# Stage one of a hybrid attention layer: later spreading of the norm factors, earlier requests for the weights of the second products, squares in groups, a longer lead for the splits

## The chip, the cores and the metric

The kernel runs on one core of a Trainium2 chip. The metric is the device time of one execution in microseconds (us). Before the change it is 1033.59 us, the median of 3 runs (1033.48 to 1034.7).

## The reference, cut to what matters

One layer is computed (DEPTH is 1): RMS norm, one input projection for query, key, value and gate, two-dimensional neighbourhood attention with a bias, a SiLU gate, an output projection with the residual, and a final RMS norm, for 2048 tokens of width 1024 and 16 heads of 64.

```python
for i in range(DEPTH):
    g, w_in, rpb, w_out = layers[i]
    h = rmsnorm(x, g)
    if i % N_MIXERS == 0:
        o, gate = neighbourhood_mixer(h, w_in, rpb)
    ...
    x = x + (o * jax.nn.silu(gate)) @ w_out
return rmsnorm(x, norm_f)
```

The change lies in the input projection `h @ w_in` for the first 1024 tokens. There `rmsnorm` is not applied to the rows first: the kernel multiplies the raw rows (times the gain `g`), and scales each finished result by its row's norm factor.

## The kernel before

**Three-part products.** Every float32 operand is split into a high part (a rounded copy, made by ScalarE, ACT in the profile) and a low part (the rest, made by VectorE, DVE). A product is then high by high, high by low and low by high on TensorE (PE). The line pairs L422/L423 (`form`, weights), L529/L530 and L526/L527 (`split_to`, the other operand) and L548/L551 (`split_v`) are such splits.

**Seven products for eight.** A product of two 2x2 block matrices is made from seven block products instead of eight (Strassen's scheme in Winograd's form). `us` in `stage_one` lists twelve weight units: four key units (n = 0 to 3), then query and gate in turn (n = 4 to 11). A unit's weights have quarters A11, A12, A21, A22 and sums S1 to S4 of them (`sum_`, L429). The rows' transposed tokens have quarters x11, x12, x21, x22 and the sums T1 to T4. `uses` says which pair each of the products P = 1 to 7 takes: 1 is A11 by x11, 2 is A12 by x21 (called here a second product; it adds to the PSUM bank of P = 1), 6 is S2 by T2, 7 is S3 by T3, 5 is S1 by T1, 4 is A22 by T4, 3 is S4 by x22. A product is 12 matmuls of 128x512 (L440), four blocks by three parts. P = 6, 7 and 4 of a unit add up in one PSUM bank; between them DVE reads the sum so far out of it (`add`, tile `u`, L453), so (n,7) has to wait until that read of (n,6) is done.

**The order in stage one** is written out by hand. `seq` lists the products of units 0 to 5: steps 0 to 3 are P = 1 of units 0 to 3, steps 4 to 7 are P = 2 of units 0 to 3, steps 8 and 9 are P = 1 and steps 10 and 11 are P = 2 of units 4 and 5. From step 12 on, ten steps make one pair of units: (0,6), (1,6), (0,7), (0,5), (1,7), (0,4), (1,5), (0,3), (1,4), (1,3) for the first pair, steps 22 to 31 for the pair (2,3), steps 32 to 41 for (4,5). From step 42 on the units go one by one. `step(i)` writes a product; what a step leaves for the other engines (copies, sums, outputs) stands behind it. `todo`, filled by `on(i, f, ...)`, hangs further work behind step i, and `forms(i + 4)` splits the weights of the coming steps, four steps ahead up to step 33, five and six after that.

**Between the first products** stand the products of the values (`first_values`, L709), the loads and splits of x12, x21, x22, the sums for T1 to T4 (`sums`, L716 to L719, and `sums4`, L724), and the norm factors. Each engine executes its instructions in the order in which they are written, and the DMA queue of SyncE (SP) too: a load that has to wait for a buffer holds up every later load and store on that queue. The SP queue also lets only a limited number of its transfers be under way, since each waits for the transfer eight places ahead of it to have landed.

**The norm factors** come in five pieces for each half c of the 1024 tokens:

- `load_rows` brings the rows in, `square_rows` squares and sums them on ACT (L209, eight instructions for each half).
- `stats` makes the reciprocal roots on DVE, fourteen small instructions (L214 to L218), into `rt` and, halved, `rth`.
- `diagonal` puts them on four diagonals on DVE (`dg`, L225) and splits these (`dgh` on ACT, L228; `dgl` on DVE, L229).
- `spread_rstd` multiplies `dgh` and `dgl` by ones on PE (L234, L235), so that every partition holds all factors, and copies the result to `rb[c]` on ACT (L238).
- `first_out` scales the sum of P = 1 and P = 2 by `rb[0]` on DVE (L353), which also frees that PSUM bank. `out_` adds up the other outputs on DVE (L458) and scales them by `rb[c]` on GpSimd (POOL, L460).

Before the change `spread_rstd(0)` stands behind step 5 and `spread_rstd(1)` behind step 8, so both come ahead of step 12. `evac_v` (L396) takes the value products out of PSUM on ACT, scaled by `rth`, and stores them (L399).

**Buffers.** `ev` is a pool of eight 128x512 tiles that many helpers share: the copies `u1v` of the first value products (L778), four of the rows of c = 1, the four `v` of `evac_v`, and `dg`, `dgh` and `dgl`. A tile can be taken again when its last user is done, which for a stored tile is the landing of the store.

Of the kernel before, what the change touches and what calls it, by code (L numbers as in the profile page):

```python
# [77 lines left out]
def build(ctx, tc, x, xr, xt, wg, bias, w_out, n0, nf, out):  # L78
    nc = tc.nc
# [327 lines left out]
    def seven_products(us, c0, X1, also):  # L407
# [3 lines left out]
        made = [0]  # L411
# [43 lines left out]
        def out_(n, a, c, P, u, then):  # L455
            kind, j = us[n]
            tmp = ev([128, 512], F32, "tmp")
            nc.vector.tensor_tensor(lay(kind, tmp), of(kind, B[n, P]), lay(kind, u), OP.add)  # L458
            if c0 == 0:
                nc.gpsimd.tensor_tensor(tmp, tmp, rb[c], OP.mult)  # L460
            then.append(lambda: give(kind, 2 * j + a, c, tmp))

# [47 lines left out]
        parts = SimpleNamespace(load=load_w, form=form, sum=sum_, product=product, keep=keep, after=after, B=B)  # L510
# [88 lines left out]
    def stage_one():  # L599
# [175 lines left out]
        split("B21", "x21", (0, 1), "x21")  # L775
        for t in range(4):
            u = ev([128, 512], F32, "u1v")
            nc.scalar.activation(u, ps[t], AF.Copy)  # L778
            nc.sync.dma_start(vu1[t], u)
# [4 lines left out]
        for n in range(2):  # L784
            seven.load(n, "A12")
        load_rows(1, range(4), ev)
# [5 lines left out]
        for n in (4, 5):  # L792
            seven.load(n, "A11")
        for k in range(4, 8):
            first_values(k)
            split("B22", "x22", (k - 4,), "x22")
            sums(k - 4)
            if k > 4:
                forms((4, 5, 7)[k - 5])
        square_rows(0, range(8))  # L800
# [4 lines left out]
        square_rows(1, range(4))  # L805
        load_rows(1, range(4, 8), mp)
        step(3)
        for t in range(4):
            evac_v(0, t, ps[t])
        forms(9)  # L810
        diagonal(0)
        split("T1", "x12", (0, 1), -1.0)
        step(4)
        for n in range(2):
            for f in ("A21", "A22"):
                seven.load(n, f)
        split("T1", "x12", (2, 3), -1.0)
        square_rows(1, range(4, 8))
        stats(1)
        step(5)  # L820
        spread_rstd(0)
        forms(11)
        split("T2", "x11", (0, 1))
        step(6)
        split("T2", "x11", (2, 3))
        diagonal(1)
        first_out(0)
        first_out(1)
        step(7)
        seven.sum(0, "S1")  # L830
        seven.sum(0, "S2")
        first_out(2)
        step(8)
        spread_rstd(1)
        forms(12)
        seven.sum(1, "S1")
        seven.sum(1, "S2")
        split("T3", "x22", (0, 1))
        step(9)
        forms(13)  # L840
        split("T3", "x22", (2, 3))
        first_out(3)
        step(10)
        seven.sum(0, "S3")
        seven.sum(1, "S3")
        forms(14)
# [5 lines left out]
        t4(0)  # L852
        step(11)
        t4(1)
        forms(15)
        on(12, t4, 2)
        on(13, t4, 3)
# [3 lines left out]
        def ask_pair(a):  # L861
            spot = mkp([128, 3, 512], F32, "raw")
            for n, f, home in ((a, "A21", spot[:, 0]), (a, "A22", spot[:, 1]), (a, "A11", spot[:, 2]), (a + 1, "A11", None)):
                seven.load(n, f, lp if home is None else lambda *_, home=home: home)

        for a in (2, 4):
            p, b = 5 * a + 2, a + 1
            on(p + 3, ask_pair, a)
            for i, n, f in ((4, b, "A21"), (4, b, "A22"), (5, a, "A12"), (6, b, "A12")):
                on(p + i, seven.load, n, f)  # L870
            for i, n, f in ((6, a, "S1"), (6, a, "S2"), (7, b, "S1"), (7, b, "S2"), (8, a, "S3"), (9, b, "S3"), (12, a, "S4"), (14, b, "S4")):
                on(p + i, seven.sum, n, f)
# [60 lines left out]
        for i in range(2 * E, N):  # L933
            step(i)
            forms(i + (4 if i < C - 8 else 5 if i < C - 5 else 6))
# [922 lines left out]
```

## Time and profile before

The profiled execution took 1033.15 us by its own time; its span on the core is 1031.4 us.

| What | Value |
|---|---|
| median of 3 runs | 1033.59 us |
| profiled execution, its own time | 1033.15 us |
| its span, mean granted TensorE clock | 1031.4 us, 0.990 |
| PE busy | 1003.2 us (97% of the span), 6904 matmuls |
| DVE busy | 781.7 us (76%) |
| ACT busy | 508.1 us (49%) |
| POOL busy | 174.2 us (17%) |

The slices of the page show where PE is not full. Each digit is a tenth of a slice's time, and a slice is 25.8 us; DVE and PEclk, the granted clock, are beside it:

```profile
PE   9779999999999999999999999999999999999997
DVE  5687788998766686667676576678888888777876
PEclk9989999999999999999999999999999999999999
```

Ahead of the last slice only the second and the third have a PE digit below 9, from 26 to 77 us, in stage one. The third also has a granted clock digit below 9.

### The profile page before, as it was taken

To read this page: it belongs to the slowest core of one execution; us is meant where nothing else is said; L and a number is where in the kernel's file an instruction comes from. 1 tells how busy PE (TensorE), PEld (TensorE's weight loads), DVE (VectorE), ACT (ScalarE), POOL (GpSimd) and SP (SyncE) were. 2 spreads that over 40 slices of the span, in tenths; PEclk is the share of its full clock that TensorE was granted. 3 is DMA by queue.
4 is the path that set the end of the run, shared out by engine and by line. 5 is a ranking of instruction groups with operands and counts; after the bars stand their busy time and mean duration, and the time that the engine had idled before them with its cause. 6 is when DMAs were issued, how large, how long until landed. Compare 5 with 4: busy or idle time off the path is not lost. (4 is left out here: it accounts for less than half of the span.)

```text
span 1031.4 us, 19603 instructions
## 1 busy us (share of the span) xinstructions
PE 1003.2 (97%) x6904; PEld 799.9 (78%) x6904; DVE 781.7 (76%) x1732; ACT 508.1 (49%) x1245; POOL 174.2 (17%) x244
## 2 busy tenths in 40 slices
PE   9779999999999999999999999999999999999997
PEld 7558778888888888888888777777777777778875
DVE  5687788998766686667676576678888888777876
ACT  7662234444335442333343466667676757563343
POOL 0001332322200000000000032323333332320100
PEclk9989999999999999999999999999999999999999
DMA  9733325787875946756555788788988679799553
GB/s 297 266 121 123 131 101 175 257 269 240 279 253 164 278 160 179 219 174 220 181 177 192 233 257 259 235 248 274 275 271 262 206 226 288 233 332 379 136 159 102
DMA packets 149834, 227.66 MB, mean 221 GB/s; under 512 B 13608, under 2 KB 65064, under 8 KB 149736
## 3 DMA queue, kind: packets, MB, share of 16 engines
q1 hardware_dynamic: 147864, 223.40, 67.4%
q0 software_dynamic: 1440, 2.62, 1.7%
q8 instruction: 54, 0.88, 0.3%
q14 instruction: 44, 0.36, 0.1%
q10 hardware_dynamic: 432, 0.40, 0.1%
HBM read 160.31 MB, written 66.06 MB: 219 GB/s over the span
## 5 line engine op out<-in xcount | busy, mean ns | idle before, releaser
L1293 POOL TENSOR_SCALAR x<-x,st 128x360 f32<-128x360 f32 (+5 forms) x192 | 106.4, 572 | 527.4 <-DVE st L1286 527.1
L440 PE MATMUL pp<-h,f 128*128 128x512 f32 x576 | 187.3, 392 | 0.0
L440 PE MATMUL pp<-t,f 128*128 128x512 f32 x702 | 172.3, 390 | 4.2 <-DVE u L453 4.2
L440 PEld LDWEIGHTS pp<-t,f 128*128 128x128 f32 x702 | 131.5, 188 | 32.6 <-issue 3.1
L1281 ACT ACTIVATE x<-x,st 128x360 f32<-128x360 f32 (+5 forms) x256 | 134.2, 526 | 26.4 <-DVE st L1275 26.4
L440 PEld LDWEIGHTS pp<-h,f 128*128 128x128 f32 x576 | 109.3, 190 | 22.9
L440 PE MATMUL pp<-l,f 128*128 128x512 f32 x288 | 113.0, 392 | 0.0
L1275 DVE CUSTOM_DVE_ANT_0 x<-s,em 128x360 f32<-128x360 f32 (+5 forms) x256 | 102.5, 454 | 1.8 <-PE s L1266 1.4
L423 DVE TENSOR_TENSOR f<-raw,f 128x512 fp32r<-128x512 f32 x105 | 77.4, 740 | 29.2 <-ACT f L422 25.3
L460 POOL TENSOR_TENSOR tmp<-tmp,rb 128x512 f32<-128x512 f32 x36 | 58.2, 1620 | 227.6 <-DVE tmp L458 103.7
L422 ACT ACTIVATE f<-raw 128x512 fp32r<-128x512 f32 x105 | 63.2, 622 | 53.1 <-DVE raw L429 29.7
L1340 PEld LDWEIGHTS o<-pta,vt 120*64 120x64 f32 (+2 forms) x1024 | 68.7, 137 | 22.7 <-DVE st L1275 15.2
L1340 PE MATMUL o<-pta,vt 120*64 120x192 f32 (+5 forms) x1024 | 83.4, 316 | 0.3 <-issue 0.3
L1310 DVE COPY pta<-ph 120x512 f32<-120x512 f32 (+5 forms) x96 | 56.0, 638 | 32.8 <-PE ph L1321 32.6
L1266 PE MATMUL s<-kt,q 64*64 64x360 f32 (+5 forms) x1024 | 78.7, 420 | 1.2 <-DVE y L1416 1.0
L1312 ACT ACTIVATE pta<-ph 120x512 f32<-120x512 f32 (+5 forms) x96 | 46.8, 558 | 62.5 <-PE ph L1321 62.3
L440 PEld LDWEIGHTS pp<-l,f 128*128 128x128 f32 x288 | 54.8, 190 | 11.6
L1266 PEld LDWEIGHTS s<-kt,q 64*64 64x64 f32 x1024 | 41.5, 131 | 23.1 <-ACT pta L1312 6.1
L594 PE MATMUL pv<-wh,t 128*128 128x512 f32 x176 | 56.2, 389 | 0.0
L440 PE MATMUL pp<-sixths,f 128*128 128x512 f32 x198 | 54.1, 397 | 0.0
L422 ACT ACTIVATE f<-s 128x512 fp32r<-128x512 f32 x42 | 26.2, 624 | 53.8 <-DVE s L429 50.5
L1626 PE MATMUL py<-woh,f 128*128 128x512 f32 x160 | 51.0, 391 | 0.9 <-DVE y L1416 0.9
(218 smaller groups left out, 1876.1 us busy)
## 6 DMA issues: line engine op xcount, KB each, us to landing
raw<-in_wg_dram SPq DMA_DIRECT2D x124, 256.0 KB, 4.9
row<-in_xr_dram SPq DMA_DIRECT2D x32, 256.0 KB, 5.1
vd<-v SPq DMA_DIRECT2D x32, 256.0 KB, 3.4
sgd<-sg SPq DMA_DIRECT2D x32, 256.0 KB, 4.4
q<-qd SPq DMA_DIRECT2D x32, 256.0 KB, 5.4
sgt<-sgd SPq DMA_DIRECT2D x32, 256.0 KB, 6.6
ogd<-og SPq DMA_DIRECT2D x32, 256.0 KB, 3.3
kt<-kd SPq DMA_DIRECT2D x16, 480.0 KB, 6.7
```

The source lines that it names most:

```text
L422: nc.scalar.activation(t[:, 0], src, AF.Copy)
L423: nc.vector.tensor_tensor(t[:, 1], src, t[:, 0].bitcast(F32), OP.subtract)
L440: nc.tensor.matmul(B[n, P], t[:, int(m == 2), c], x[k][int(m == 1)], start=P in (1, 6, 5) and k == 0 and m == 0, stop=k == 3 and m == 2, s ...
L460: nc.gpsimd.tensor_tensor(tmp, tmp, rb[c], OP.mult)
L594: nc.tensor.matmul(p, a[:, o], b, start=P in (1, 6, 5) and k == 0 and m == 0, stop=k == 3 and m == 2, skip_group_check=True)
L1266: nc.tensor.matmul(pst[s][h * 64:h * 64 + 64], qt[a, g * 64:g * 64 + 64], kt[a, :r1 - r0, c0:c0 + 8 * WIDE[C]].rearrange("p r (s c) -> p s ...
L1275: nc.vector.tensor_tensor_reduce(X[i, C][s], pst[s], EM[p, ROW_TYPE[T]][C > 0][s], -1.0, 1e38, OP.add, OP.min, st[:, o:o + 1])
L1281: nc.scalar.activation(X[i, C][s], X[i, C][s], AF.Exp, bias=st[:, o:o + 1], scale=-1.0, accum_out=st[:, 4 + o:5 + o])
L1293: nc.gpsimd.tensor_scalar(X[i, C][s], X[i, C][s], st[:, o:o + 1], 1.0, op0=OP.mult, op1=OP.mult)
L1310: nc.vector.tensor_copy(o, i_)
L1340: nc.tensor.matmul(o[s * 64:s * 64 + 64, g0 * 64:g1 * 64], vt[:k, strip, s * 64:s * 64 + 64], t[:k, n * 64:(n + g1 - g0) * 64], start=stri ...
L1626: nc.tensor.matmul(B[m, P], t[:, a, c], b, start=P in (1, 6, 5) and k == 0 and i == 0, stop=k == 3 and i == 2, skip_group_check=True)
```

## The change

The diff moves calls in the hand-written order; no arithmetic is added or left out.

- `load` of A12 of units 0 and 1 goes ahead of the stores of `u1v` and of the rows' loads; the rows of c = 1 are asked for behind the A12 and A11 of units 2 to 5, the first six instead of the first four.
- The squares of c = 0 are written in two groups of four among the sums of x12 and x22. The squares of c = 1 go behind `diagonal(0)`, behind steps 4 and 5.
- `spread_rstd(0)` goes from behind step 5 to behind step 8, three products later. `spread_rstd(1)` goes from behind step 8 to behind step 15. One output of step 15 that needs `rb[1]` is held until step 16 (`held`, `scale_held`).
- `stats(1)` goes from behind step 4 to behind step 9, the sums S1, S2 and S3 of units 0 and 1 and the splits of T1, T2, T3 move by a step or two, and all four pieces of T4 go behind steps 12 to 15.
- The loads and sums of the pairs (2,3) and (4,5) get a table `d` of their own steps.
- The splits of the weights (`forms`) run four steps ahead up to step 16, five up to 20, and six from 21 on.

Three places show the new order, each as it was and as it is now. The line numbers of the changed kernel are some ten higher from L500 on (L526 is L536, L779 is L791, L628 is L638).

First the DMA queue of SP, from the loads of x12 and x22 (`land`) to the stores of the value products (`vd`). `raw` are weights, `row` the rows for the norm, `vu` the stores of `u1v`. Before:

```order
L519 DMA land<-in_xt_dram 128x512 x8
L779 DMA vu_93<-u1v 128x512 x4
L628 DMA row<-in_xr_dram 128x512 x8
L417 DMA raw<-in_wg_dram 128x512 x2
L628 DMA row<-in_xr_dram 128x512 x4
L417 DMA raw<-in_wg_dram 128x512 x6
L628 DMA row<-in_xr_dram 128x512 x4
L399 DMA vd_83<-v 128x4x128 x4
L417 DMA raw<-in_wg_dram 128x512 x4
```

Now:

```order
L529 DMA land<-in_xt_dram 128x512 x8
L417 DMA raw<-in_wg_dram 128x512 x2
L791 DMA vu_93<-u1v 128x512 x4
L638 DMA row<-in_xr_dram 128x512 x8
L417 DMA raw<-in_wg_dram 128x512 x4
L638 DMA row<-in_xr_dram 128x512 x6
L417 DMA raw<-in_wg_dram 128x512 x2
L638 DMA row<-in_xr_dram 128x512 x2
L417 DMA raw<-in_wg_dram 128x512 x4
L399 DMA vd_83<-v 128x4x128 x4
```

The two A12 (`raw x2`) moved ahead of `vu` and the rows, and the four loads of A21 and A22 (`raw x4`, the last ones) moved ahead of the stores `vd`.

Second ACT, from the value outputs `v` to the copies `p` of the sums of steps 8 and 9. Before:

```order
L396 ACTIVATE v<-pv,rth 128x512 x4
L422 ACTIVATE f<-raw 128x512 x2
L228 ACTIVATE dgh<-dg 128x512
L529 ACTIVATE t<-land 128x512 x4
L209 ACTIVATE row,ss<-row 128x512 x4
L238 ACTIVATE rb<-prb 128x512
L422 ACTIVATE f<-raw 128x512 x2
L526 ACTIVATE t<-land 128x512 x4
L228 ACTIVATE dgh<-dg 128x512
L448 ACTIVATE p_788<-pp 128x512
```

Now:

```order
L396 ACTIVATE v<-pv,rth 128x512 x4
L228 ACTIVATE dgh<-dg 128x512
L209 ACTIVATE row,ss<-row 128x512 x4
L539 ACTIVATE t<-land 128x512 x4
L422 ACTIVATE f<-raw 128x512 x2
L209 ACTIVATE row,ss<-row 128x512 x4
L536 ACTIVATE t<-land 128x512 x4
L448 ACTIVATE p_753<-pp 128x512
L238 ACTIVATE rb<-prb 128x512
```

All eight squares of c = 1 now stand between the first `dgh` and the first `p`, the copy of `rb` behind that `p`, and the second `dgh` no longer ahead of it.

Third DVE at the diagonals of c = 0, with the semaphores that a row waits for (DMAHW are landed transfers). Before:

```order
L423 TENSOR_TENSOR f<-raw,f 128x512 [waits DMAHW6_49,PE_49,Activation_49]
L423 TENSOR_TENSOR f<-raw,f 128x512 [waits DMAHW7_49,PE_49,Activation_49]
L225 TENSOR_SCALAR dg<-ident,rt 128x128 [waits Pool_49]
L225 TENSOR_SCALAR dg<-ident,rt 128x128 x3
L229 TENSOR_TENSOR dgl<-dg,dgh 128x512 [waits Activation_49]
L530 SCALAR_TENSOR_TENSOR t<-land,t 128x512 [waits Activation_49] x4
```

Now:

```order
L423 TENSOR_TENSOR f<-raw,f 128x512 [waits DMAHW2_49,PE_49,Activation_49]
L423 TENSOR_TENSOR f<-raw,f 128x512 [waits DMAHW3_49,PE_49,Activation_49]
L225 TENSOR_SCALAR dg<-ident,rt 128x128 [waits DMAHW2_49,DMAHW4_49,Activation_49,Pool_49]
L225 TENSOR_SCALAR dg<-ident,rt 128x128 x3
L229 TENSOR_TENSOR dgl<-dg,dgh 128x512 [waits DMAHW6_49,DMAHW4_49,Activation_49]
L540 SCALAR_TENSOR_TENSOR t<-land,t 128x512 [waits Activation_49] x4
```

`dg` and `dgl` now wait for transfers too: they take `ev` tiles of `v`, and the transfers are the stores of these (and the earlier stores of `u1v` from the same tiles).

The diff:

```diff
@@ -408,7 +408,7 @@
         seq = [(n, P) for n in range(len(us)) for P in order7]
         last = len(us) - 1
         A, F, B, U = {}, {}, {}, {}
-        made = [0]
+        made, held = [0], []
 
         def load_w(n, f, home=raw):
             A[n, f] = home([128, 512], F32, "raw")
@@ -456,9 +456,19 @@
             kind, j = us[n]
             tmp = ev([128, 512], F32, "tmp")
             nc.vector.tensor_tensor(lay(kind, tmp), of(kind, B[n, P]), lay(kind, u), OP.add)
-            if c0 == 0:
-                nc.gpsimd.tensor_tensor(tmp, tmp, rb[c], OP.mult)
+            def scale():
+                if c0 == 0:
+                    nc.gpsimd.tensor_tensor(tmp, tmp, rb[c], OP.mult)
+
+            if c0 == 0 and c not in rb:
+                held.append(lambda: (scale(), give(kind, 2 * j + a, c, tmp)))
+                return
+            scale()
             then.append(lambda: give(kind, 2 * j + a, c, tmp))
+
+        def scale_held():
+            while held:
+                held.pop(0)()
 
         def ahead(i, lead=6):
             n, j = divmod(i, 7)
...
@@ -773,6 +783,8 @@
         split_v(0, 0, 2)
         split_v(0, 1, 2)
         split("B21", "x21", (0, 1), "x21")
+        for n in range(2):
+            seven.load(n, "A12")
         for t in range(4):
             u = ev([128, 512], F32, "u1v")
             nc.scalar.activation(u, ps[t], AF.Copy)
@@ -781,9 +793,6 @@
         step(0)
         split_v(0, 0, 3)
         split_v(0, 1, 3)
-        for n in range(2):
-            seven.load(n, "A12")
-        load_rows(1, range(4), ev)
         split("B21", "x21", (2, 3), "x21")
         step(1)
         forms(3)
@@ -791,85 +800,90 @@
             seven.load(n, "A12", sp)
         for n in (4, 5):
             seven.load(n, "A11")
+        load_rows(1, range(4), ev)
+        load_rows(1, range(4, 6), mp)
         for k in range(4, 8):
             first_values(k)
             split("B22", "x22", (k - 4,), "x22")
             sums(k - 4)
-            if k > 4:
-                forms((4, 5, 7)[k - 5])
-        square_rows(0, range(8))
+            if k == 5:
+                forms(5)
+            if k > 5:
+                square_rows(0, range(4 * k - 24, 4 * k - 20))
+        forms(7)
         stats(0)
         step(2)
         for n in (4, 5):
             seven.load(n, "A12", sp)
-        square_rows(1, range(4))
-        load_rows(1, range(4, 8), mp)
+        load_rows(1, range(6, 8), mp)
         step(3)
+        forms(9)
         for t in range(4):
             evac_v(0, t, ps[t])
-        forms(9)
-        diagonal(0)
-        split("T1", "x12", (0, 1), -1.0)
-        step(4)
         for n in range(2):
             for f in ("A21", "A22"):
                 seven.load(n, f)
+        diagonal(0)
+        step(4)
+        square_rows(1, range(4))
+        split("T1", "x12", (0, 1), -1.0)
+        step(5)
         split("T1", "x12", (2, 3), -1.0)
+        forms(11)
         square_rows(1, range(4, 8))
-        stats(1)
-        step(5)
+        step(6)
+        for n in range(2):
+            for f in ("S1", "S2"):
+                seven.sum(n, f)
+        split("T2", "x11", (0, 1))
+        step(7)
+        split("T2", "x11", (2, 3))
+        step(8)
         spread_rstd(0)
-        forms(11)
-        split("T2", "x11", (0, 1))
-        step(6)
-        split("T2", "x11", (2, 3))
-        diagonal(1)
+        forms(12)
+        step(9)
+        forms(13)
         first_out(0)
         first_out(1)
-        step(7)
-        seven.sum(0, "S1")
-        seven.sum(0, "S2")
+        stats(1)
+        step(10)
+        split("T3", "x22", (0, 1))
+        for n in range(2):
+            seven.sum(n, "S3")
+        forms(14)
         first_out(2)
-        step(8)
-        spread_rstd(1)
-        forms(12)
-        seven.sum(1, "S1")
-        seven.sum(1, "S2")
-        split("T3", "x22", (0, 1))
-        step(9)
-        forms(13)
+        step(11)
         split("T3", "x22", (2, 3))
+        forms(15)
         first_out(3)
-        step(10)
-        seven.sum(0, "S3")
-        seven.sum(1, "S3")
-        forms(14)
 
         def t4(*ks):
             sums4(*ks)
             split("T4", "x21", ks)
 
-        t4(0)
-        step(11)
-        t4(1)
-        forms(15)
-        on(12, t4, 2)
-        on(13, t4, 3)
+        for k in range(4):
+            on(12 + k, t4, k)
+        on(13, diagonal, 1)
+        on(15, spread_rstd, 1)
+        on(16, seven.scale_held)
         on(14, seven.sum, 0, "S4")
         on(16, seven.sum, 1, "S4")
 
         def ask_pair(a):
             spot = mkp([128, 3, 512], F32, "raw")
-            for n, f, home in ((a, "A21", spot[:, 0]), (a, "A22", spot[:, 1]), (a, "A11", spot[:, 2]), (a + 1, "A11", None)):
-                seven.load(n, f, lp if home is None else lambda *_, home=home: home)
+            for i, f in enumerate(("A21", "A22", "A11")):
+                seven.load(a, f, lambda *_: spot[:, i])
 
         for a in (2, 4):
             p, b = 5 * a + 2, a + 1
-            on(p + 3, ask_pair, a)
-            for i, n, f in ((4, b, "A21"), (4, b, "A22"), (5, a, "A12"), (6, b, "A12")):
-                on(p + i, seven.load, n, f)
-            for i, n, f in ((6, a, "S1"), (6, a, "S2"), (7, b, "S1"), (7, b, "S2"), (8, a, "S3"), (9, b, "S3"), (12, a, "S4"), (14, b, "S4")):
-                on(p + i, seven.sum, n, f)
+            d = (14, 13, 16, 17, 17, 16, 19, 20, 22, 24) if a == 2 else (23, 24, 26, 28, 25, 27, 28, 30, 32, 34)
+            on(d[0], ask_pair, a)
+            for f in ("A21", "A22", "A11"):
+                on(d[1], seven.load, b, f)
+            for i, n in ((2, a), (3, b)):
+                on(d[i], seven.load, n, "A12")
+            for i, n, f in ((4, a, "S1"), (4, a, "S2"), (5, b, "S1"), (5, b, "S2"), (6, a, "S3"), (7, b, "S3"), (8, a, "S4"), (9, b, "S4")):
+                on(d[i], seven.sum, n, f)
         for n in range(E, len(us)):
             b = C + 7 * (n - E)
             d = (-9, -6 if n == E else -7, -7, -6, -5, -3)
@@ -932,7 +946,7 @@
         on(N - 1, load_s, "S3", 2, 3)
         for i in range(2 * E, N):
             step(i)
-            forms(i + (4 if i < C - 8 else 5 if i < C - 5 else 6))
+            forms(i + (4 if i < 17 else 5 if i < 21 else 6))
 
         def give_v(u, t, p, add):
             v = ev([128, 512], F32, "v")
```

More of the change, by code (lines that the diff above doesn't have):

```diff
@@ L508, in run @@
                 f()
-        parts = SimpleNamespace(load=load_w, form=form, sum=sum_, product=product, keep=keep, after=after, B=B)
+        parts = SimpleNamespace(load=load_w, form=form, sum=sum_, product=product, keep=keep, after=after, scale_held=scale_held, B=B)
         return ahead, run, parts
```

## The prediction

> **What bounds the kernel now.** I first read the busy times in stretches of 25 us. Columns: stretch, length, then busy time and instructions of PE, weight load, DVE, ACT and POOL, then granted clock, DMA share, GB/s.
>
> ```profile
> 25.00:50.00 25.00, 19.14 (x85) 15.52 (x83) 16.38 (x34) 15.21 (x39) 0.00 (x0) 0.96 0.77 263
> 50.00:75.00 25.00, 17.70 (x61) 13.50 (x62) 19.14 (x47) 16.80 (x36) 0.00 (x0) 0.76 0.44 148
> 75.00:100.00 25.00, 24.50 (x109) 19.98 (x108) 20.52 (x33) 7.41 (x13) 4.01 (x3) 1.00 0.34 116
> 100.00:125.00 25.00, 23.19 (x103) 18.89 (x102) 18.20 (x24) 5.87 (x10) 7.60 (x5) 1.00 0.37 128
> 125.00:150.00 25.00, 23.14 (x96) 18.69 (x95) 18.69 (x25) 6.69 (x12) 8.34 (x5) 0.93 0.32 104
> 150.00:175.00 25.00, 25.00 (x112) 20.70 (x111) 21.70 (x31) 10.60 (x19) 9.09 (x6) 1.00 0.43 133
> ```
>
> From 150 us on, the bound is PE: 112 matmuls in 25 us, 0.223 us each. A product of 12 is then 2.7 us. The change's reach ends there; what it saves earlier moves everything later forward by as much. Between 25 and 150 us there are 27 + 51 + 3 + 9 + 16 = 106 matmuls fewer than five times 112, which is 23.7 us. That is the most it can win.
>
> Next, the timeline of PE: start, duration, row, in brackets the idle time before it and its releaser.
>
> ```profile
> 43.76 0.39 PE L440 MATMUL pp<-h,f 128*128 128x512 f32 x1
> 55.21 0.79 PE L234 MATMUL prb<-dgh,onesr 128*128 128x512 f32 x1 [11.07 <-ACT dgh L228]
> ...
> 67.61 0.49 PE L234 MATMUL prb<-dgh,onesr 128*128 128x512 f32 x1 [1.85 <-ACT dgh L228]
> ...
> 84.58 0.93 PE L440 MATMUL pp<-t,f 128*128 128x512 f32 x3 [0.50 <-DVE u L453]
> ...
> 113.86 0.93 PE L440 MATMUL pp<-t,f 128*128 128x512 f32 x3 [1.81 <-DVE u L453]
> ...
> 143.20 1.19 PE L440 MATMUL pp<-t,f 128*128 128x512 f32 x3 [1.86 <-DVE u L453]
> ```
>
> Five waits, 17.1 us. Two are for the diagonals of `spread_rstd`, three for DVE to read a bank (steps 14, 24 and 34). The rest of the 23.7 us is clock; the same columns for the stretches behind four of the waits:
>
> ```profile
> 55.20:58.60 3.40, 3.39 (x8) 2.42 (x9) 3.09 (x5) 3.40 (x9) 0.00 (x0) 0.54 0.92 295
> 67.60:72.10 4.50, 4.25 (x11) 3.12 (x12) 4.37 (x7) 2.31 (x5) 0.00 (x0) 0.62 0.33 120
> 113.80:117.30 3.50, 3.44 (x15) 2.88 (x16) 2.11 (x4) 0.00 (x0) 0.00 (x0) 1.00 0.23 77
> 143.20:147.60 4.40, 4.40 (x12) 3.47 (x13) 2.25 (x4) 1.15 (x2) 0.00 (x0) 0.61 0.84 251
> ```
>
> The clock lost is 3.4 x 0.46 = 1.6, 4.5 x 0.38 = 1.7 and 4.4 x 0.39 = 1.7 us. Behind 113.86 nothing was lost.
>
> Why `dgh` was late stands in the timelines of ACT, DVE and SP's queue (in this order).
>
> ```profile
> 36.02 0.63 ACT L422 ACTIVATE f<-raw 128x512 fp32r<-128x512 f32 x1 [9.47 <-DMA raw<-in_wg_dram]
> ...
> 45.40 0.61 ACT L209 ACTIVATE row<-row 128x512 f32<-128x512 f32 x1
> ...
> 49.41 2.39 ACT L396 ACTIVATE v<-pv,rth 128x512 f32<-128x512 f32 x4
> ...
> 54.53 0.63 ACT L228 ACTIVATE dgh<-dg 128x512 fp32r<-128x512 f32 x1 [1.69 <-DVE dg L225]
> 55.07 2.17 ACT L529 ACTIVATE t<-land 128x512 fp32r<-128x512 f32 x4
> 57.15 0.61 ACT L209 ACTIVATE row<-row 128x512 f32<-128x512 f32 x1
> ...
> 59.60 0.58 ACT L238 ACTIVATE rb<-prb 128x512 f32<-128x512 f32 x1
> 60.08 1.14 ACT L422 ACTIVATE f<-raw 128x512 fp32r<-128x512 f32 x2
> ```
> ```profile
> 44.10 1.29 DVE L423 TENSOR_TENSOR f<-raw,f 128x512 fp32r<-128x512 f32 x2
> 46.14 0.16 DVE L214 TENSOR_TENSOR m<-ss 128x4 f32<-128x4 f32 x1 [0.75 <-ACT row L209]
> ...
> 48.71 0.17 DVE L218 TENSOR_SCALAR rth<-rt 128x4 f32<-128x4 f32 x1
> ...
> 53.57 0.87 DVE L225 TENSOR_SCALAR dg<-ident,rt 128x128 f32<-128x128 f32 x4
> ...
> 113.03 0.68 DVE L453 TENSOR_TENSOR u<-pp,acc 128x512 f32<-128x512 f32 x1
> ```
> ```profile
> 20.36 3.15 SPq L779 DMA_DIRECT2D vu<-u1v  x4
> 25.17 5.34 SPq L628 DMA_DIRECT2D row<-in_xr_dram  x8
> 30.84 1.23 SPq L417 DMA_DIRECT2D raw<-in_wg_dram  x2
> 34.74 11.00 SPq L417 DMA_DIRECT2D raw<-in_wg_dram  x6
> ...
> 50.11 2.42 SPq L399 DMA_DIRECT2D vd<-v  x4
> ```
>
> ACT stood still for 9.47 us for A12 of unit 0, which SP asked for at 30.84, behind four stores and eight rows. Then came the squares (to 46.0), the statistics (to 48.9), the value outputs (49.41), the diagonals (53.57).
>
> **The change, part by part.** *A12 earlier.* It is now issued where the stores were, from 20.36. Landings of transfers issued about then and when the queue is less full, KB and us:
>
> ```profile
> vu<-u1v SPq DMA_DIRECT2D x4, 256.0 KB, 7.2
> land<-in_xt_dram SPq DMA_DIRECT2D x1, 256.0 KB, 7.9
> ...
> vd<-v SPq DMA_DIRECT2D x4, 256.0 KB, 4.2
> raw<-in_wg_dram SPq DMA_DIRECT2D x20, 256.0 KB, 5.2
> ```
>
> So it lands at 28.3 instead of 36.0. The rows slip by two places of 5.34 / 8 = 0.67 us, so the first arrives at 25.17 + 1.3 + 5.2 = 31.7 (by the last row). ACT's four splits and sums take it to 31, four squares to 34.3, two more to 35.6, four squares to 38.1, and the splits of A12 of units 2 and 3, whose loads follow the rows (31.8 + 5.2 = 37.0), to 39.3. DVE ends its share at 40.5, not 45.4. The squares cost no new time, as they now fill a stretch in which ACT waited. The statistics (46.14 to 48.88, 2.7 us) follow at once and end at 43.2, 5.7 us earlier.
>
> *The diagonal waits for a store.* The rows of c = 1 now still hold their four `ev` tiles when `dg` is written, so `dg` takes the tile of the first `v`, and `dgh` and `dgl` those of the next two: they wait until these are stored. With the stores the loads of A21 and A22 move ahead in the queue, and two of those wait for DVE's splits behind the statistics (43.2 + 1.3 = 44.5). The first store is issued at 44.8. It lands 4.2 us later, by its own row, or 5.2, by the loads that lie ahead of it: 49.0 to 50.0; I take 49.5. `dg` is then ready at 50.4, `dgh` at 51.0 and `dgl` at 51.7. The 5.7 us have shrunk to 3.9 at `dgh` (54.53 + 0.63 = 55.2 before).
>
> *The spread three products later.* PE ends step 5 at 44.0 as before. Steps 6 to 8 have their splits by 44.5 and end at 52.2. The spread finds `dgh` and `dgl` ready: the 11.07 us wait is gone. Step 9 ends at 55.3. But step 10 adds to the bank of step 8, which ACT has to copy first (`p`, L448), and that copy stands behind eight squares, eight splits of T1 and T2 and two of weights. By the rows above four squares take 59.60 - 57.15 = 2.45 us, four splits 2.1, two 1.0: 2 x 2.45 + 2 x 2.1 + 1.0 = 10.1. From 51.0 that is 61.1, with the copy 61.7. **PE now waits 6.4 us at step 10**, instead of 11.07 at the spread, and will run at half clock behind it.
>
> *DVE's chain to step 24.* From here DVE is the pace: its queue holds T1's and T2's low parts, sums, `first_out`, `stats(1)`, T3, T4, `diagonal(1)`, and only then `u` of step 22, which releases step 24. Its busy time in that stretch before:
>
> ```profile
> 45.40:113.70 68.30, 54.24 (x220) 43.12 (x220) 53.29 (x106) 32.89 (x68) 9.94 (x6) 0.90 0.37 121
> ```
>
> So 53.3 us of work and 15.0 idle. The change makes the work two operations longer (splits that now run ahead; 1.2 us). I count its idle time: 44.5 to 49.5 for the store (5.0), 0.7 for `dgh`, 2.3 for ACT's squares ahead of T1, and seven handovers between ACT and DVE at 0.75, as ahead of L214 (5.2): 13.2. So `u` ends at 40.5 + 53.3 + 1.2 + 13.2 = 108.2; with the idle time of before, 110.0. I take 109, so step 24 starts at 109.1 instead of 113.86: **4.8 us won**. The shorter waits of PE in between (at steps 14, 17 and the second spread, by my count 1.5 to 2.5 each) and their clock lie inside this chain and cost nothing more.
>
> *The longer lead behind step 24.* From there to `u` of step 32 DVE has 28 operations before and now, 19 us at 0.68 each; the stretch from 100 to 125 us, of the same mix and with POOL's multiplies beside it, has 18.2 us of DVE in 25. Ten steps are 27 us of PE, so DVE can catch up. Before, sums and the splits that need them stood directly in front of that `u`; now they stand a step or two ahead. I expect no wait at step 34: 1.86 + 1.7 of clock, **3.5 us won**. If the chain stays late, nothing. The held output and the moved loads cost nothing: the new pair loads are issued over ten us ahead of their sums, and one POOL multiply fewer is in the way at step 15.
>
> *The clock behind short waits.* The rows show it halved behind waits of 1.85 and 1.86 us, not behind 1.81. I charge nothing for one behind step 24 and keep 1.7 us as the end of the range. By the Trainium skill, page "TensorE: Matmul & The Clock Gate", Part 1, the clock halves only after an idle window of about 3.4 us. By that page only the wait at step 10 would be followed by half clock, and the half clock at 143.20 would have another cause and could stay, which would make the sum 6.6 us instead of 8.3. The trace here disagrees with it in two cases of three.
>
> **The sum.** 4.8 + 3.5 = 8.3 us off the profiled execution's 1033.15 gives 1024.9; that execution lies 0.4 below the median of the runs, so I say 1025.
>
> **The rivals.**
>
> - *DVE does not hold the later steps.* Then only the wait at step 10 and its clock are left, 6.4 + 1.6 of the 17.1 + 5.0, and the gain is 14: 1019. For it: DVE is busy only 18 to 20 us of 25 between 75 and 150 us. Against: its operations stand in one queue behind a start at 51.7.
> - *The wait at step 34 stays*, or a half clock comes behind step 24: 4.8 minus 0 to 1.7 is won, 1028.3 to 1030. For it: DVE reaches step 24 as the last one again, as before.
> - *The store lets the diagonal wait much longer.* Place: the first store behind four loads on SP. Price: each us past 49.5 moves `dgh`, the copy for step 10, DVE's chain and step 24 by one. From 57.8 on the gain is used up, and with three more the time is 1036. For it: nothing releases ACT or DVE meanwhile, as both have the diagonal as their next instruction. Against: a landing of 13 us where no row above has over 7.9.
> - *Nothing comes of it*: DVE's chain loses in handovers what its start won, and step 34 waits as before: 1033.
>
> **How the numbers follow.** The forecast has a chance of 0.50, with its own range of 1023 to 1028 (store at 48 to 52, idle time of 13 to 15). DVE not binding has 0.14, the wait at step 34 staying 0.20, no change 0.06, the late store 0.10. The range leaves out most of the last two and the far half of the first rival: 1019 to 1031. About 0.2% (2 us) is what a measurement of this kernel can tell from no change. Faster: 0.50 + 0.14 + 0.20 = 0.84. Within it 0.06, slower 0.10.
>
> **What would show it.** Right: ACT's gap at 26 to 36 us shrinks to about 2; L234 runs at about 52 with no wait; PE's longest gap is ahead of step 10, released by ACT's `p`, 5 to 8 us; DVE and ACT idle together at 45 to 50 until `vd` lands; step 24 starts near 109. Wrong: a gap ahead of the first L234, no gap at step 10, a wait at 136 to 140 released by `u`, or PE not dense behind 150.

## The result, and the profile after

The changed kernel takes 1029.27 us, the median of 9 runs (1027.36 to 1033.33); the kernel before takes 1033.48 us in 9 runs of the same session (1032.29 to 1037.7). The ratio is 0.9958 (95% interval 0.9938 to 0.9978): faster by 4.2 us, where 8.3 were forecast. Two later sessions gave 0.9944 (0.9925 to 0.9963) and 0.9939 (0.9926 to 0.9952), which is 6.0 us in each, so the change is worth 4 to 6 us.

The profiled execution happens to be the slowest of the nine: 1033.33 us. PE's busy time and the granted clock by stretches (the columns as in the prediction):

```profile
25.00:50.00 25.00, 25.00 (x112) 20.71 (x111) 17.83 (x37) 16.26 (x35) 0.00 (x0) 1.00 0.98 342
50.00:75.00 25.00, 17.74 (x61) 13.45 (x60) 18.20 (x43) 15.76 (x37) 0.00 (x0) 0.80 0.22 70
75.00:100.00 25.00, 21.99 (x92) 16.80 (x91) 20.95 (x35) 7.57 (x14) 2.58 (x2) 1.00 0.34 114
100.00:125.00 25.00, 22.13 (x90) 17.51 (x88) 20.82 (x27) 6.40 (x11) 8.77 (x6) 0.93 0.41 141
125.00:150.00 25.00, 25.00 (x112) 20.72 (x111) 19.60 (x29) 7.56 (x13) 9.43 (x6) 1.00 0.30 104
```

From 25 to 50 and from 125 on PE is now full (112 matmuls; 85 and 96 before). From 75 to 125 it does 30 matmuls less than before. Its longest waits there, from the timeline of PE (start, duration, row, idle time before it and its releaser):

```profile
54.55 0.50 PE L234 MATMUL prb<-dgh,onesr 128*128 128x512 f32 x1 [2.00 <-ACT dgh L228]
...
65.14 0.79 PE L440 MATMUL pp<-h,f 128*128 128x512 f32 x1 [5.03 <-ACT p L448]
...
92.54 0.49 PE L440 MATMUL pp<-t,f 128*128 128x512 f32 x1 [1.22 <-ACT t L536]
...
113.53 1.44 PE L440 MATMUL pp<-t,f 128*128 128x512 f32 x3 [1.97 <-DVE u L453]
```

The 11 us wait for the first diagonal has become 2 us there and 5 us at step 10, and the wait at step 34 is gone. But step 24 starts at 113.53, and started at 113.86 before. Why stands in the timelines of SP's queue, ACT and DVE:

```profile
44.31 2.56 SPq L417 DMA_DIRECT2D raw<-in_wg_dram  x4
46.99 3.01 SPq L399 DMA_DIRECT2D vd<-v  x4
```
```profile
29.67 1.33 ACT L422 ACTIVATE f<-raw 128x512 fp32r<-128x512 f32 x2 [2.87 <-DMA raw<-in_wg_dram]
...
44.49 2.42 ACT L396 ACTIVATE v<-pv,rth 128x512 f32<-128x512 f32 x4 [1.37 <-DVE rth L218]
53.87 0.63 ACT L228 ACTIVATE dgh<-dg 128x512 fp32r<-128x512 f32 x1 [6.96 <-DVE dg L225]
```
```profile
44.28 0.17 DVE L218 TENSOR_SCALAR rth<-rt 128x4 f32<-128x4 f32 x1
...
52.91 0.87 DVE L225 TENSOR_SCALAR dg<-ident,rt 128x128 f32<-128x128 f32 x4 [7.23 <-DMA vd<-v]
```

The norm factors are ready at 44.45, 4.4 us earlier than before (48.88). DVE then does two more splits and ACT the value outputs, and after that both stand still for 7 us, until the first store of `v` has landed and its tile can take `dg`.

A second profile of the same kernel (1028.54 us, the run called again below) is nearer to the median. Its timelines of SP's queue, ACT, DVE and PE at the same places:

```profile
19.95 1.20 SPq L417 DMA_DIRECT2D raw<-in_wg_dram  x2
...
44.53 2.75 SPq L399 DMA_DIRECT2D vd<-v  x4
```
```profile
42.27 2.42 ACT L396 ACTIVATE v<-pv,rth 128x512 f32<-128x512 f32 x4 [1.51 <-DVE rth L218]
```
```profile
50.23 0.88 DVE L225 TENSOR_SCALAR dg<-ident,rt 128x128 f32<-128x128 f32 x4 [6.76 <-DMA vd<-v]
...
54.82 2.50 DVE L540 SCALAR_TENSOR_TENSOR t<-land,t 128x512 fp32r<-128x512 f32 x4 [2.28 <-ACT t L539]
```
```profile
62.45 0.80 PE L440 MATMUL pp<-h,f 128*128 128x512 f32 x1 [6.60 <-ACT p L448]
...
110.86 0.94 PE L440 MATMUL pp<-t,f 128*128 128x512 f32 x3 [1.95 <-DVE u L453]
111.63 3.81 PE L440 MATMUL pp<-sixths,f 128*128 128x512 f32 x9
```

Here stage one is 2.2 us ahead of the first profile already at the value outputs (42.27, 44.49), and 2.7 us at `dg` and at step 24. SP's queue has the 2.2 us from the request for the two A12 on, at 19.95 here and at 22.14 in the first profile. The 2.00 us that PE waits at the first spread in the first profile are gone here. In both profiles, nine matmuls behind step 24 take about twice their time; the granted clock of the 4 us there is 0.63 in the second profile:

```profile
110.80:114.80 4.00, 3.94 (x11) 3.16 (x12) 2.31 (x4) 1.15 (x2) 0.00 (x0) 0.63 0.84 168
```

### The profile page after: what moved, and what is told of

Its sections match the earlier page's. It is cut to its first block, busy times and chain, and to the rows that moved or that the text cites. A ratio compares the mean times of both kernels' runs of the same rounds, so it can differ in the third digit from the quotient of the medians.

```text
span 1031.6 us, 19605 instructions
## 1 busy us (share of the span) xinstructions
PE 1005.6 (97%) x6904; PEld 800.5 (78%) x6904; DVE 782.8 (76%) x1732; ACT 508.0 (49%) x1245; POOL 174.6 (17%) x244
## 5 line engine op out<-in xcount | busy, mean ns | idle before, releaser
L1335 PEld LDWEIGHTS ph<-ident,x 64*120 64x120 f32 (+2 forms) x1408 | 42.5, 128 | 11.3 <-issue 9.5
```

## The experiments

The medians and the ratios to the kernel before, which ran beside each; the four lines of a block are one session.

| Run | Median, us | Ratio (95%) |
|---|---|---|
| again (changed kernel) | 1028.89 | 0.9944 (0.9925 to 0.9963) |
| squares_first | 1023.43 | 0.9891 (0.9869 to 0.9913) |
| old_lead | 1032.2 | 0.9974 (0.9957 to 0.9991) |
| dve_more | 1031.36 | 0.9964 (0.9949 to 0.9979) |
| copy_first | 1028.37 | 0.9930 (0.9913 to 0.9948) |
| no_scale | 1025.63 | 0.9902 (0.9883 to 0.9922) |
| sums_ahead | 1016.75 | 0.9826 (0.9805 to 0.9847) |
| a12_alone (on the kernel before) | 1035.32 | 0.9999 (0.9985 to 1.0012) |
| after_beside (changed kernel) | 1028.64 | 0.9939 (0.9926 to 0.9952) |
| spread_back | 1032.57 | 0.9981 (0.9970 to 0.9992) |
| stats_later | 1018.17 | 0.9837 (0.9823 to 0.9852) |
| copy_too | 1018.61 | 0.9838 (0.9822 to 0.9855) |

The kernel before had 1034.93, 1035.62 and 1034.61 us in the three sessions.

**again: the changed kernel once more.**

> The changed kernel once more, nothing edited, for a second profile. Its runs so far lie at 1027.4 to 1033.3 us with granted clocks of 0.990 to 0.995, and the profiled execution was the slowest of them: behind step 24 it ran at half clock, and its lead over the kernel before fell from 2.4 us at 800 us to nothing at 945. Theory A (the plan of stage one is the same in each execution, and what differs is how many short waits of PE are followed by half clock, 1.6 to 1.8 us each): the waits of PE stand at the same places within 1 us (spread about 2, step 10 about 5, step 24 about 2, none at step 34), the first vd store lands at 51.5 to 53, dgh ends at 53.5 to 54.7, and a faster execution differs by its clock alone: 1029 us at 0.993. Rival B (the landings differ, and the store lands early in the faster executions): an execution at 1028 shows the store at 49.5 to 50.5, dgh at 51 to 52 and step 24 at 109 to 110.

Both are partly right. From step 10 on the waits stand at the same places, but the landing of the store moves from execution to execution (52.9 and 50.2), and step 24 with it. Little of that is the store itself, which holds `dg` for 5.9 and 5.7 us behind its issue: most of the 2.7 us lies ahead of it, on SP's queue. What makes that queue late is not shown. The rest between the two profiles lies behind stage one: the wait of 1.01 us near 838 is followed by a low clock in the slower one (see the last section), and at 950 the slower one waits 1.11 us for a split of ACT.

**squares_first: is it the store?** The four `ev` tiles of the rows are given back before the diagonal needs tiles.

```diff
+        square_rows(1, range(4))
         diagonal(0)
         step(4)
-        square_rows(1, range(4))
```

> The squares of the first four rows of c = 1 stand ahead of diagonal(0), so that their ev tiles are given back and dg, dgh and dgl take them instead of the tiles of the stored v. The rows land at 43.0 to 45.0 and ACT has nothing to do from 46.9 to 53.9. Theory A (the one wait for the vd stores is what shrank the gain): no instruction waits for vd any more, dgh ends at about 50 instead of 54.5, the first spread waits less than 0.3 us, the wait at step 10 shrinks from 5.0 to 2 to 4 us, as the four squares no longer stand behind dgh, and step 24 starts at 107 to 110 instead of 113.5: a time of 1023 to 1026. Rival B (the later steps are set by something else, such as the DVE operations that POOL's multiplies slow down, or handovers): dgh is early, but step 24 stays at 112 to 114 and the time at 1028 to 1030.

`dg` now waits for ACT's square alone, and step 24 comes 6.2 us sooner than in the second profile of the changed kernel, sooner than expected. DVE and PE:

```profile
45.84 0.87 DVE L225 TENSOR_SCALAR dg<-ident,rt 128x128 f32<-128x128 f32 x4 [1.94 <-ACT row L209]
```
```profile
56.27 0.50 PE L440 MATMUL pp<-h,f 128*128 128x512 f32 x1 [1.03 <-ACT p L448]
...
69.74 0.94 PE L440 MATMUL pp<-t,f 128*128 128x512 f32 x3 [2.29 <-DVE u L453]
...
104.68 0.94 PE L440 MATMUL pp<-t,f 128*128 128x512 f32 x3 [1.96 <-DVE u L453]
105.45 2.23 PE L440 MATMUL pp<-sixths,f 128*128 128x512 f32 x9
```

Theory A holds: 5.5 us off the changed kernel's time in the same session. Of the 6.2 us at step 24, `dg` gives 4.4; the other 1.8 go with the four squares, which no longer stand between the diagonal and T1's splits: DVE's wait of 2.28 us there is gone, and its wait ahead of `dgl` grew from 0.74 to 1.40 us. PE's wait at step 10 fell too, from 6.60 to 1.03 us. That this is not what moved step 24 can be read from DVE's rows: between `dg` and the `u` of step 22 all its waits are for ACT, and none for PE, in this run and in the changed kernel. Behind the wait of 1.96 us the clock stayed full here: nine matmuls in 2.23 us instead of 3.81.

**dve_more: does DVE's queue set step 24?**

```diff
-        nc.vector.tensor_tensor(l, dg, h.bitcast(F32), OP.subtract)
+        for _ in range(4 if c == 1 else 1):
+            nc.vector.tensor_tensor(l, dg, h.bitcast(F32), OP.subtract)
```

> In diagonal(1), step 13, the subtraction that makes dgl is done four times instead of once: three more operations of 0.69 us on DVE, 2.1 us in all, with the same result. Theory A (DVE's queue from the first dgl to u of step 22 sets the start of step 24): that u ends 2.1 us later, step 24 starts at 115.3 to 115.9 instead of 113.5, and the time is 1.5 to 2.5 us above the changed kernel's of the same call. Rival B (DVE has slack there, for instance since its waits for ACT and PE absorb it): step 24 moves by less than 0.8 us and the time by less than 0.8 us.

Theory A: 2.5 us more, for 2.1 us of added work, and step 24 came 62.8 us behind `dg` instead of 60.6. (It starts at 113.36, not at 115.3 to 115.9, since `dg` stands at 50.55 here, and the expectation went by the first profile with `dg` at 52.91.) PE waits 2.41 us for the longer `dgl` at the second spread, but DVE's rows behind `dgl` show no wait for PE, so the added work reached step 24 by DVE's queue.

```profile
50.55 0.88 DVE L225 TENSOR_SCALAR dg<-ident,rt 128x128 f32<-128x128 f32 x4 [6.76 <-DMA vd<-v]
```
```profile
113.36 0.93 PE L441 MATMUL pp<-t,f 128*128 128x512 f32 x3 [1.95 <-DVE u L454]
```

**old_lead: what is the longer lead worth?** The loads and sums of the pairs and `forms` as before (the table of the diff undone):

```diff
-            forms(i + (4 if i < 17 else 5 if i < 21 else 6))
+            forms(i + (4 if i < C - 8 else 5 if i < C - 5 else 6))
```

> The changed kernel with the loads, sums and the lead of splits for units 2 to 5 as before (pair loads at p + 3 to p + 6, sums at p + 6 to p + 14, lead 4 up to C - 8). Theory A (the longer lead won the wait at step 34): PE waits 1.5 to 2.5 us at step 34 for u again, with half clock behind it in some executions, the steps up to 24 stay within 1 us, and the time is 2 to 3.5 us above the changed kernel's in the same call: 1031 to 1033 for 1029. Rival B (step 34 lost its wait because of the earlier spreads, not of the lead): no wait at step 34 and the same time within 1 us.

The wait at step 34 is back; the time rises by 3.3 us. (The profiled execution, at 1029.90 us, is one of the fastest of its twelve and shows full clock behind both waits.) PE:

```profile
112.34 0.94 PE L440 MATMUL pp<-t,f 128*128 128x512 f32 x3 [3.24 <-DVE u L453]
...
141.67 0.93 PE L440 MATMUL pp<-t,f 128*128 128x512 f32 x3 [1.85 <-DVE u L453]
```

**copy_first: does the wait at step 10 cost anything?**

```diff
-        split("T2", "x11", (2, 3))
         step(8)
+        split("T2", "x11", (2, 3))
         spread_rstd(0)
```

> The changed kernel with the second half of T2's splits behind step 8, so that the copy p (L448) for which step 10 waits stands in front of four splits on ACT instead of behind them. Theory A (the wait at step 10 lies inside DVE's chain and costs nothing): the wait at step 10 shrinks from 5.0 to 6.6 us to 3 to 4.5, the time thus won is waited for later (at steps 14, 17, 21 or 24), step 24 starts within 1 us of the changed kernel's, and the time is within 1 us of it, 1028 to 1030. Rival B (the wait at step 10 and the half clock behind it are on the path): the time falls by the same 2 us, to 1026.5 to 1027.

It shrank by less than expected, to 5.58 us, and the 1.0 us won there is given back by step 24, which starts at 111.26, with `dg` at 50.63 (again 60.6 apart). The time is that of the changed kernel: theory A, as far as 1 us can tell. PE:

```profile
61.82 0.79 PE L440 MATMUL pp<-h,f 128*128 128x512 f32 x1 [5.58 <-ACT p L448]
...
111.26 1.12 PE L440 MATMUL pp<-t,f 128*128 128x512 f32 x3 [1.95 <-DVE u L453]
```

**spread_back: is the moved spread worth anything by itself?** The two matmuls and the copy `rb` of the first spread go back behind step 5.

```diff
         step(5)
+        spread_rstd(0)
...
         step(8)
-        spread_rstd(0)
```

> The changed kernel with the first spread (two matmuls and the copy rb) back behind step 5, where it stood before; all else as changed. Theory A (DVE's chain from the first dgl sets step 24, so where PE waits ahead of it does not matter): PE waits 7 to 9 us at the first spread instead of 0 to 2, the wait at step 10 shrinks by as much, to 0 to 1 us, step 24 starts within 1 us of the changed kernel's, and the time is within 1.2 us of it. Rival B (the three products that PE does ahead of the spread are won time): step 24 and the time come 4 to 7 us later, 1033 to 1035.

Neither theory had it right: 3.9 us more than the changed kernel beside it, just short of B's range. PE waits 10.07 us at the spread again, and step 24 starts 63.4 us behind `dg` (51.90 to 115.33), not 60.6. The rows of DVE say where most of the 2.8 us are lost:

```profile
51.90 0.87 DVE L225 TENSOR_SCALAR dg<-ident,rt 128x128 f32<-128x128 f32 x4 [7.85 <-DMA vd<-v]
...
66.17 0.69 DVE L423 TENSOR_TENSOR f<-s,f 128x512 fp32r<-128x512 f32 x1 [0.61 <-ACT f L422]
68.89 0.69 DVE L423 TENSOR_TENSOR f<-s,f 128x512 fp32r<-128x512 f32 x1 [2.03 <-ACT f L422]
```

ACT makes those `f` behind its copies `p`, and the copies have to wait for steps 8 and 9, which are now late on PE. So DVE's chain is not free of PE: through ACT's queue it waits for the products ahead of step 10. The rest of the 4.3 us at step 24 is the store: it was issued 1.5 us later in this execution than in the one beside it (46.09, there 44.62), and `dg` stands at 51.90, there at 50.35. Whether that is so in the median execution too, one profile cannot tell. The one beside it is a third profile of the changed kernel:

> The changed kernel beside the next three, as their measure: 1027 to 1030 us; the wait at step 10 at 5 to 6.7 us with half clock behind it, the wait at step 24 at 1.9 to 2.0 us, with half clock behind it or not.

Its waits are 6.62 us at step 10 and 1.96 us at step 24, which starts at 111.00, 60.65 us behind `dg`, with a low clock behind both (0.50 and 0.71 in the next 3 us).

**a12_alone: the early load on the kernel before.**

```diff
+        for n in range(2):
+            seven.load(n, "A12")
         for t in range(4):
             u = ev([128, 512], F32, "u1v")
...
-        for n in range(2):
-            seven.load(n, "A12")
         load_rows(1, range(4), ev)
```

> The kernel before with one part of the change alone: the loads of A12 of units 0 and 1 ahead of the stores of u1v and of the rows. Theory A (this load is what made the first diagonal late, and DVE's chain carries its lead on to step 24): ACT's gap at 26 to 36 us shrinks from 9.5 to about 2, dgh ends at 50 to 52 instead of 55.2, the wait at the first spread is 6 to 8 us instead of 11.1, step 24 starts at 109.5 to 111.5 instead of 113.9, the wait at step 34 stays at 1.8 to 2, and the time is 3 to 4.5 us below the kernel before. Rival B (moving the spread behind PE's products is what saves): dgh earlier, but less than 1.5 us off the time.

Both fall: nothing is won at all. ACT's gap for A12 of units 0 and 1 shrinks from 9.47 to 1.79 us, and the next load makes a new one of 8.55. ACT and SP's queue:

```profile
27.63 0.63 ACT L422 ACTIVATE f<-raw 128x512 fp32r<-128x512 f32 x1 [1.79 <-DMA raw<-in_wg_dram]
...
39.79 1.27 ACT L422 ACTIVATE f<-raw 128x512 fp32r<-128x512 f32 x2 [8.55 <-DMA raw<-in_wg_dram]
```
```profile
26.25 7.49 SPq L628 DMA_DIRECT2D row<-in_xr_dram  x12
34.04 8.16 SPq L417 DMA_DIRECT2D raw<-in_wg_dram  x6
```

Twelve rows stand ahead of the A12 of units 2 and 3, and ACT's squares stand behind the splits of these. In the changed kernel those four rows stand behind these weights, and the squares ahead of the splits. That this is what makes the load pay was not run on its own.

**no_scale: do POOL's multiplies slow DVE?** The outputs of units 0 and 1 are left unscaled.

```diff
-                if c0 == 0:
+                if c0 == 0 and n > 1:
                     nc.gpsimd.tensor_tensor(tmp, tmp, rb[c], OP.mult)
```

> The changed kernel without POOL's multiplies of the outputs of units 0 and 1 by the norm factors (those outputs are left unscaled): six multiplies of 1.3 to 1.7 us between 90 and 112 us are gone. In that stretch seven operations of DVE take 1.2 to 1.8 us instead of 0.68, about 4.5 us in all, each beside such a multiply. Theory A (they are slowed by it, and they stand in the chain that sets step 24): the DVE operations between 90 and 112 take 0.68 us each, u of step 22 ends 3 to 4.5 us earlier, the wait at step 24 is gone or under 0.5 us, as PE can be there 1.95 us earlier at most without its other waits, and the time is 2 to 4 us below the changed kernel's: 1025 to 1027. Rival B (they are long for another reason): durations and time stay, 1028.5 to 1029.5.

Theory A: 3.0 to 3.3 us below the changed kernel's medians in the sessions before and after, as the changed kernel did not run beside this one, and no wait of PE at step 24. The same two DVE steps with the multiplies (the first profile of the changed kernel) and without:

```profile
99.27 1.66 DVE L429 TENSOR_TENSOR s<-s,raw 128x512 f32<-128x512 f32 x1
...
110.42 2.36 DVE L423 TENSOR_TENSOR f<-raw,f 128x512 fp32r<-128x512 f32 x2
```
```profile
96.80 0.69 DVE L429 TENSOR_TENSOR s<-s,raw 128x512 f32<-128x512 f32 x1
...
105.13 1.28 DVE L423 TENSOR_TENSOR f<-raw,f 128x512 fp32r<-128x512 f32 x2
```

**sums_ahead, stats_later, copy_too: a faster kernel.** On top of squares_first, each sum for T4 goes one step ahead of its split:

```diff
-        def t4(*ks):
-            sums4(*ks)
-            split("T4", "x21", ks)
+        def t4(k):
+            if k < 3:
+                sums4(k + 1)
+            split("T4", "x21", (k,))
+
+        sums4(0)
```

> The kernel with the squares first (1023.4 us in its runs), and each sum for T4 one step ahead of its split: DVE then no longer waits 0.70 to 0.76 us for ACT in front of each of the four splits. Theory A (handovers in DVE's chain set steps 14 to 24): four waits of 0.73 us go, 2.9 us; the waits of PE at step 14 (2.29) and step 24 (1.96) shrink together by 1.5 to 2.9 us, and the time is 1020.5 to 1022. Rival B (POOL's multiplies and the splits in front of u decide on their own): step 24 moves by less than 0.5 us, 1023 to 1024.

More than theory A expected: 1016.75 us, 1.7% below the kernel before. With the four handovers gone, PE's wait at step 24 is gone too. The one profile, of the slowest of five executions (1020.94 us), starts step 24 about 3 us sooner than squares_first; where the rest of the 6.7 us between the two medians lies, it does not show. Two waits in stage one are left:

```profile
56.74 0.50 PE L440 MATMUL pp<-h,f 128*128 128x512 f32 x1 [1.22 <-ACT p L448]
...
70.88 1.62 PE L440 MATMUL pp<-t,f 128*128 128x512 f32 x3 [2.92 <-ACT t L536]
```

The wait at step 14 is put down to ACT's split; the operations that DVE has ahead of its `u` of step 12 are the other candidate, and were tried next, by `on(12, stats, 1)` in place of `stats(1)` behind step 9:

> The kernel with squares first and sums ahead (1016.8 us in its runs), and the 14 small operations of stats(1), 3 us on DVE, behind u of step 12 instead of ahead of it. Theory A (DVE's queue ahead of that u is the whole of the 2.9 us wait at step 14): that wait is under 0.6 us, the second diagonal is later but its spread still waits under 1 us, and the time is 1 to 3 us lower: 1013.5 to 1015.5. Rival B (the work only moves the wait): the wait comes again at the second spread, step 17 or 24, 1.5 to 3 us, and the time stays at 1016 to 1017.5.

```profile
67.99 0.94 PE L440 MATMUL pp<-t,f 128*128 128x512 f32 x3 [0.31 <-ACT t L536]
...
75.72 0.49 PE L234 MATMUL prb<-dgh,onesr 128*128 128x512 f32 x1 [2.01 <-ACT dgh L228]
...
101.01 0.93 PE L440 MATMUL pp<-t,f 128*128 128x512 f32 x3 [0.66 <-DVE u L453]
```

PE's rows show theory B: the wait at step 14 fell to 0.31 us, so DVE's operations were its cause, but the second spread now waits 2.01 us and step 24 0.66, and the ratio cannot be told from the last one (the median of 1018.17 lies 0.7 us above the range of B). In copy_too the edit of copy_first comes on top:

> As the last one, and the second half of T2's splits behind step 8, so that the copy p stands in front of them on ACT. Theory A (with DVE ahead of PE, a wait of PE for ACT is now on the path): the wait at step 10 (1.2 us) goes, and the time is 0.5 to 1.2 us below the last one's. Rival B: the splits of T2 then come late, steps 12 to 14 wait for them or for DVE instead, and the time is the same within 0.5 us or higher.

The wait at step 10 (1.4 us in stats_later) went, step 14 waits 1.31 instead of 0.31, and the ratio is the same: theory B. The three kernels are equal within their intervals, and the simplest of them, sums_ahead, is the one to keep.

## Why the prediction was right, and where its size was off

The time of 1029.27 lies in the range, 4.3 us above the forecast. It lies outside the narrower range that the prediction gave to its main case (1023 to 1028) and within that of its second rival (1028.3 to 1030), which the full range took in; by the medians of each session, 4.2 to 6.0 us were won of the 8.3. In the second profile, which is near the median, the steps come out as follows.

- *A12 and the squares* (statistics end at 43.2): 42.2, in the first profile 44.45. The mechanism was right, but a12_alone shows that the early load alone is not enough.
- *The diagonal waits for a store* (lands at 49.5, `dgh` ready at 51.0): `dg` starts at 50.23, `dgh` ends at 51.8. The first store was issued when expected (44.53), yet `dg`, which waits for its landing, starts 5.7 us later, not 4.2 to 5.2; in the first profile it was 5.9 (46.99 to 52.91). What squares_first took away, 4.4 us at `dg` and 5.5 us of the time, is the price of this wait with the four squares behind it.
- *The wait at step 10* (6.4 us): 6.60, 5.03 in the first profile. That it costs nothing is what copy_first says, within 1 us, for the 1.0 us that it took away.
- *The waits at 14, 17 and the second spread lie inside DVE's chain*: yes; dve_more moves step 24 by its added work.
- *Step 24 at 109.1, 4.8 us won*: this is the term that was mis-sized. Step 24 starts at 110.86, 3.0 us sooner than before. The chain from `dg` to step 24 takes 60.6 us in each profile that leaves it alone (52.91 to 113.53, 50.23 to 110.86, 50.63 to 111.26), where 59.6 were counted, and the store took the other 0.7. Counted over the whole chain, from the end of DVE's share (39.5, 40.5 was expected) to the `u` of step 22 (110.7), DVE worked 55.1 us and stood idle for 16.1, where 54.5 and 13.2 were counted: the work was about right and the idle time too small, 1.8 us of it ahead of `dg` (6.76 instead of 5.0).
- *The longer lead, 3.5 us won*: old_lead gives 3.3.
- *No charge for the clock behind step 24*: this is the other term. The prediction kept 1.7 us for it as the end of its range, and that was the case: at a clock of 0.63 for 4 us it is 4 x 0.37 = 1.5 us.

With these sizes the sum is 3.0 + 3.5 - 1.5 = 5.0 us off 1033.15, 1028.2, and that execution took 1028.54. So the forecast's mechanism held, with the half clock that stood among the second rival's cases, and with less won at step 24. One of its signs of being wrong, a gap ahead of the first L234, was there in the first profile (2.00 us) and not in the second, in which `dg` was 2.7 us earlier. That moving the spread earns nothing by itself, which followed from the claim that DVE alone sets the pace, is wrong: spread_back loses 2.8 us at step 24 for a reason that was not seen, the copies `p` on ACT.

## What to carry to other kernels

When a step is made early, look at which buffer it takes next: a tile that still waits for a store's landing hands back the time, and using up another tile first (here by moving one line) won 5.5 us, about as much as the whole change (4.2 to 6.0). On an engine whose queue sets the pace, count the handovers, not only the work: four waits of 0.75 us for a neighbour's half of a split went by writing the next sum ahead of them. A load moved forward alone can only expose the next load behind it, as in a12_alone.

## What the runs showed of the hardware

**Low clock behind short waits does not follow from their length.** In the fourteen profiles all ten waits of PE of 5 us or more in and behind stage one were followed by half clock (0.50 in the 3 us behind them); of the 23 between 1.6 and 3.3 us, 15 were followed by 0.50 to 0.83 and 8 by a full clock, among them the longest (3.24, old_lead). The same wait of 1.01 us near 838 was followed by it in the first profile of the changed kernel and not in the second:

```profile
838.50:842.50 4.00, 3.83 (x32) 2.10 (x32) 3.41 (x14) 3.81 (x12) 0.00 (x0) 0.78 0.71 228
```
```profile
836.30:840.30 4.00, 3.84 (x42) 2.19 (x44) 3.58 (x14) 3.85 (x12) 0.00 (x0) 1.00 0.75 234
```

So a short wait taken away saves its clock only in some executions; what decides it is not shown. The spread of the changed kernel's times (1027.4 to 1033.3) is only in part this clock: of the 4.8 us between its first two profiles 2.2 are there ahead of 838 us, and these go back to SP's late queue. The Trainium skill, page "TensorE: Matmul & The Clock Gate", Part 1, speaks of a free-running window and of differences between executions, which fits; an idle window of about 3.4 us as the condition does not fit waits of 1.0 to 2.9 us with half clock behind them.

**A multiply of POOL slows DVE, but not every operation.** Beside a multiply of POOL, DVE's operations on two SBUF tiles took 0.9 to 1.8 us instead of 0.68, while `tmp<-pp,u`, with one operand in PSUM, stayed at 0.68. Rows of POOL and DVE in the first profile of the changed kernel:

```profile
103.06 3.39 POOL L461 TENSOR_TENSOR tmp<-tmp,rb 128x512 f32<-128x512 f32 x2 [2.68 <-DVE tmp L458]
```
```profile
103.49 0.68 DVE L458 TENSOR_TENSOR tmp<-pp,u 128x512 f32<-128x512 f32 x1
104.09 1.19 DVE L429 TENSOR_TENSOR raw<-raw 128x512 f32<-128x512 f32 x1
```

The Trainium skill, page "SBUF — State Buffer", section "Who interferes with whom", says that a DVE instruction with two SBUF inputs contends with a GpSimd instruction that reads SBUF. The trace agrees: 1.66 us with and 0.69 us without.
